# Hybrid diffusion step on one core: layer 0's S5 preparation in S5's own pages and banks, S5's output left where it is made, the retention's values elsewhere

## The chip, the cores and the metric

The kernel runs on one core of a Trainium2 chip. The metric is the device time of one execution in microseconds (us). The core has five engines that work side by side, each through its own queue in a fixed order: TensorE (PE: matmuls and transposes), VectorE (DVE), ScalarE (ACT), GpSimd (POOL), and SyncE (SP), which issues the DMAs here. SBUF is the on-chip memory, PSUM the accumulator memory of TensorE with eight banks.

## The reference

A backbone of two layers runs over two request groups at once: a prompt of 128 tokens and a sample of 512, side by side as 640 columns. Each layer modulates a normed input, projects it once, hands slices of the projection to four mixers, joins their outputs in one projection, and adds a gated feed-forward network.

```python
mod = silu(cond) @ mod_w + mod_b                 # six shifts, scales, gates
h = rmsnorm(x, norm1_w) * (1 + sc1) + sh1
pa, pb, pc, pd = split(h @ w_in)
ya, st_a = ssd_mixer(pa, ...)                    # chunked scan, two directions
yb, st_b = retention_mixer(pb, ...)              # chunked decay attention, two directions
yc, st_c = s5_mixer(pc, ...)                     # complex diagonal scan
yd, st_d = lru_mixer(pd, ...)                    # gated diagonal scan
x = x + g1 * (concatenate([ya, yb, yc, yd]) @ w_out)
h = rmsnorm(x, norm2_w) * (1 + sc2) + sh2
x = x + g2 * conv_ffn(h, ffn_w_up, ffn_conv_w, ffn_conv_b, ffn_w_down)
```

S5 is the mixer that the change is about. Its state matrices follow from parameters alone (`lam`, `log_step`, `b`, `c`), so they can be worked out before any input is there:

```python
step = exp(log_step); mag = exp(lr * step)
abar = mag * (cos(li * step) + 1j * sin(li * step))
bbar = (abar - 1) / lam * b
x = complex_diag_scan(abar, einsum(u, bbar), init)       # both directions
y = real(einsum(x, c)) + d_skip * u
val, gate = split(y @ glu_w);  out = val * sigmoid(gate)
```

The outputs are both groups' final hidden states and the new states of the four mixers.

## The kernel before

Activations lie with features on the partitions and the 640 tokens along the free axis, in two halves of 320. Products of float32 are made of three matmuls: each operand is split into a high part of reduced precision and the rest (names `hi`, `lo`; for the normed input `hhi`, `hlo`), and a tile is the sum of high by high, high by low and low by high. A tile of the input projection is 2 x 8 x 3 such matmuls of 320 columns, named `mm<-hhi,hi` and so on.

**Pages and banks.** SBUF work space is cut into pages of one size under tags, and PSUM into banks under tags; `page(tag)` and `paged(tag, shape, name)` take the next page of a tag, `bank(tag)` the next bank:

```python
PAGES = {"A": 12, "B": 12, "C": 12, "Ya": 2, "Yb": 2, "Yc": 2, "Yd": 2, "H": 16}
BANKS = {"mm": 3, "a": 1, "b": 2, "c": 1, "mod": 1}
```

A is used by the LRU mixer, B by S5, C by SSD; Ya, Yb, Yc and Yd hold the outputs of LRU, SSD, S5 and retention. Bank a serves the LRU, b S5 and the retention, c SSD, mm the large products. A scheduler sets the order of each engine's queue ahead of the run, by program order as priority; the helper `call` (its line is 92, and every instruction of the trace has that line) adds one rule: the first instructions on the tiles of one tag come in program order. So a stage that takes pages of a tag early in the program also comes ahead of every later stage that takes pages of this tag.

**Layer 0's mixers.** In `layer`, the S5 input is projected first (`u`), then `s5_prep(0)` is written out, and then the steps of the mixers in the order of `ORDER[0]`. The prep makes powers of the poles (`pw`, `apcw`), tables (`tab`, stored to DRAM as `tb`), and, in four rounds of four groups, `pmr`/`pmi` from `bb`, their transposes (`wbs`, stored as `wb`), the products `kt` and `kk` with `cm`, and `pmr`/`pmi` from `cq` (stored as `wc`). At its end `dg` is made of `kk`, and both are stored as `zz`. The mixer loads them back in eight scans q0 to q7: matmuls `b<-s5u,wb`, products with the tables (`s5a<-b,tb` on VectorE), two scan instructions (`s5r<-tb,s5a`), products back, then matmuls with `wc`. After q7 come the transposes into `s5y`, the gated unit (`b<-s5y,glu`, tanh into `glut`), and the output.

The other names: `lgw` are LRU's gate matmuls, `gb` its gelu gate; `sxc`, `scb`, `sE`, `xk`, `ssq` belong to SSD, with `z` its gate and `yssd` its output; `rq`, `rv`, `ktok`, `qe`, `rM` belong to the retention; `mod<-mraw` are the modulation's matmuls, written as fillers over the whole mixer stage. The mixers' outputs are split into `yhi` and `ylo`, and the first matmul `mm<-yhi,hi` begins the output projection: first LRU and S5, then SSD and retention.

Of the kernel before, what the change touches and what calls it, by code (L numbers as in the profile page):

```python
# [29 lines left out]
NF = 22  # L30
TB = 81
SK = 2
PB = "c"
EXTRA = ''
TBA = 1
PCP = 1
# [2 lines left out]
TSR = 1  # L39
LB = 1  # L40
FPS = 2
ST = 'AAC'
MR = 'C'

ORDER = ("s5 gb lru lru gb ssd ssd z lru ssd z ret ret ssd ret ssd ret ret ret ret",
# [30 lines left out]
def hybrid_kernel(ctx: ExitStack, tc: tile.TileContext, I, O, dbg=None):  # L76
# [33 lines left out]
    V, G, A, T, SP = Eng(nc.vector), Eng(nc.gpsimd), Eng(nc.scalar), Eng(nc.tensor), Eng(nc.sync)  # L110
# [15 lines left out]
    def page(tag, dt=F32, name="pg"):  # L126
        t = pgp.tile([P, PGB if tag == "B" else PGW], dt, tag=tag, name=name, bufs=PAGES[tag])
        fresh[t.tensor.name] = tag
        return t

    def paged(tag, shape, name, dt=F32):
        n = int(np.prod(shape))
        t = page(tag, dt, name)[:, :n]
        if len(shape) == 1:
            return t
        names = "abcd"[:len(shape)]
        return t.rearrange(f"p ({' '.join(names)}) -> p {' '.join(names)}", **dict(zip(names[1:], shape[1:])))

    def bank(tag):
        t = psp.tile([P, 512], F32, tag=tag, name=tag, bufs=BANKS[tag])  # L140
        fresh[t.tensor.name] = tag
        return t
# [43 lines left out]
    def wsplit(ap, n, cut=512, le=None, tag=None):  # L186

        out = []
        for c0 in range(0, n, cut):
            w = min(cut, n - c0)  # L190
            raw = wp.tile([P, 512], F32, tag="raw", name="raw", bufs=RAWS)
            SP.dma_start(raw[:, :w], ap[:, c0:c0 + w])
            if tag:
                hi, lo = page(tag, F32R, "whi")[:, :512], page(tag, F32R, "wlo")[:, :512]
            else:
                hi = wp.tile([P, 512], F32R, tag="hi", name="hi", bufs=SPLITS)
                lo = wp.tile([P, 512], F32R, tag="lo", name="lo", bufs=SPLITS)
            A.copy(hi[:, :w], raw[:, :w])
            lo_i[0] += 1
            (le or lo_eng[lo_i[0] % len(lo_eng)]).tensor_tensor(lo[:, :w], raw[:, :w], r2f(hi[:, :w]), op=ALU.subtract)  # L200
            out.append((c0, c0 + w, hi, lo))
        return out
# [11 lines left out]
    def col_tile(w, act, nk=8, width=128, halves=(0, 1), col=None, ks=None, out=None):  # L214

        col = col or (lambda k: k * width)
        some = ks or range(nk)
        old = sec[0]
        sec[0] = old + "*"
        out = [out] if out is not None else [bank("mm") for _ in halves]  # L220
        for c0, c1, hi, lo in w:
            ks = [k for k in some if c0 <= col(k) < c1]
            for ps, h in zip(out, halves):
                o, n = HALF[h]
                for k in ks:
                    c = slice(col(k) - c0, col(k) - c0 + width)
                    mm3(ps[:width, :n], hi[:, c], lo[:, c], act[k][0][:, o:o + n], act[k][1][:, o:o + n],
                        k == 0, k == nk - 1)
        sec[0] = old
        return out  # L230
# [261 lines left out]
    M_, A_, S_ = ALU.mult, ALU.add, ALU.subtract  # L492
# [99 lines left out]
    def s5_prep(l):  # L592

        wb, wc, tb, zz = s5d[l]
        p1, p2, p3 = "CCC" if l else ST

        def keep(name, shape):
            return smp.tile([P] + shape, F32, tag=f"k_{name}", name=name)
# [19 lines left out]
        tp = paged(p1, [2, 2, 16, 4], "pwt")  # L618
# [3 lines left out]
        for n in (1, 2, 4):  # L622
            v, o = pwp[:, :, :, 1:1 + n], pwp[:, :, :, 1 + n:1 + 2 * n]
            b = pwp[:, :, :, n:n + 1]
            t, u = [tp[:, i, :, :, 0:n] for i in range(2)]
# [38 lines left out]
            G.tensor_copy(s5x0[l][DH[d], :, :, d].rearrange("p g i -> p i g"), x0[DH[d]])  # L664
        yield


        ek = [u8]
        for k in range(1, 6):
# [4 lines left out]
        for q in range(2):  # L674
            o = 8 * q
# [4 lines left out]
            for k in range(6):  # L680
                n = 1 << k
# [7 lines left out]
            for h in range(2):  # L689

                rv = paged(p1, [4, 2, TB], "tbr")
                for i in range(2):
                    t = tab[i][:, 4 * h:4 * h + 4, :]
# [25 lines left out]
             [bb[:, i] for i in range(2)], [bt[:, i] for i in range(2)])  # L719
        ncq = paged(p2, [16, 16], "ncq")  # L720
        V.tensor_scalar(ncq, cq[:, 1], -1.0, None, op0=M_)
        cm = [paged(p2, [16, 32], f"cm{i}") for i in range(2)]
        for i, c in enumerate((cq[:, 0], ncq)):
            G.memset(cm[i], 0.0)
            for d in range(2):
# [5 lines left out]
        for q in range(4):  # L731
            o = 4 * q
# [15 lines left out]
            for i in range(2):  # L748
                ps = bank("c" if l else PB)
                for k in range(4):  # L750
# [3 lines left out]
                for a in range(2):  # L754
                    SP.dma_start(wb[2 * q + a].rearrange("p (g i c) -> p g i c", g=2, i=2)[:, :, i, :], wbs[:, a])
            ps = bank("c" if l else PB)
            for i in range(2):
# [4 lines left out]
            A.copy(kt, ps[:, 0:128])  # L762
            ps = bank("c" if l else PB)
            T.transpose(ps[:, 0:128], kt, idn)
# [26 lines left out]
    def s5_mixer(l, hh, y, steps):  # L791
# [3 lines left out]
        for i in range(2):  # L795
# [9 lines left out]
            ps = bank("b")  # L805
# [3 lines left out]
            ps = bank("b")  # L809
            for k in range(2):  # L810
                for j in range(2):
                    o = 256 * k + 128 * j
# [111 lines left out]
        for i in range(2):  # L924
            tp = page("B", name="glut")
            for h in range(2):
                o, n = HALF[h]
                t = tp[:, o:o + n]
                for vg in (1, 0):
                    ps = bank("b")  # L930
                    for k in range(2):
                        m = 256 * vg + 128 * i
                        T.matmul(ps[:, :n], gw[k][:, m:m + 128], yt[k][:, o:o + n], start=k == 0, stop=k == 1)
                    if vg:
                        A.activation(t, ps[:, :n], AF.Tanh, scale=0.5)
                    else:
                        V.scalar_tensor_tensor(t, t, 1.0, ps[:, :n], op0=A_, op1=M_)
                G.tensor_scalar(y[i][:, o:o + n], t, 0.5, None, op0=M_)


    def lru_mixer(l, hh, y):
# [296 lines left out]
    def ret_mixer(l, hh, y):  # L1238
# [60 lines left out]
        kx = rotated(13)  # L1299
        yield  # L1300
        units = wsplit(I["w_in"][l, 14], 1024) + wsplit(I["w_in"][l, 15], 1024)
        vk = [paged("B", [5, 128], "rv") for _ in range(2)]
        for c0 in (0, 2, 4):
            n = min(2, 5 - c0)
            ps = bank("b")
            old = sec[0]
            sec[0] = old + "*"
            for c in range(n):
                for k in range(8):
                    hi, lo = units[k // 2][2:]  # L1310
                    w = slice((k % 2) * 256, (k % 2) * 256 + 256)

                    mh, ml = [v[:, 128 * (c0 + c):128 * (c0 + c) + 128] for v in hh[k]]
                    o = ps[:, 256 * c:256 * c + 256]
                    T.matmul(o, mh, hi[:, w], start=k == 0, stop=False)
                    T.matmul(o, mh, lo[:, w], start=False, stop=False)
                    T.matmul(o, ml, hi[:, w], start=False, stop=k == 7)
            sec[0] = old
            for i in range(2):
                A.copy(vk[i][:, c0:c0 + n], ps[:, 0:256 * n].rearrange("p (c w) -> p c w", w=256)[:, :, 128 * i:128 * i + 128])  # L1320
# [16 lines left out]
        for t in range(2):  # L1337
            sq, sp = page("A", name="rsq"), page("A", name="rsp")
            for h in range(2):
                o, n = HALF[h]  # L1340
                ps = bank("b")
# [3 lines left out]
                ps = bank("b")  # L1345
# [14 lines left out]
    def layer(l, norm):  # L1360
# [3 lines left out]
        for ks in steps or (range(8),):  # L1364
            if l == 0 and ks[0]:
                mod_first(ks[0] // 2)
            for h in HO:
                norm.apply(l, 0, h, hh, ks)
        normed = hold[1]
        ys = {n: [page(tag, name="y" + n) for _ in range(2)] for n, tag in (("lru", "Ya"), ("ssd", "Yb"), ("s5", "Yc"))}  # L1370
        ys["ret"] = []
        gens = {"s5": s5_mixer(l, hh, ys["s5"], steps), "lru": lru_mixer(l, hh, ys["lru"]), "ssd": ssd_mixer(l, hh, ys["ssd"]),
                "ret": ret_mixer(l, hh, ys["ret"]), "gb": gates(l, hh, (2, 3), ys["lru"], AF.Gelu_apprx_tanh),
                "z": gates(l, hh, (9, 11), ys["ssd"], None if TSZ else AF.Silu)}
        for n in gens:
            if n != "ret":
                step(n + str(l), gens[n])
            if l == 0 and n == "s5":
                step("s50", gens[n])
                sec[0] = "prep"  # L1380
                for i, _ in enumerate(s5_prep(0)):
                    if i == 1:

                        hold[0] = normed
                hold[0] = None
# [45 lines left out]
        for h in HO:  # L1431
            for m in range(8):
                if m not in us:
                    us[m] = wsplit(I["w_o2"][l, m], 512, tag="C" if m < 4 else None)
                ps = pss.pop(m) if m in pss else col_tile(us[m], act, nk=4, halves=(h,))[0]
# [3 lines left out]
        f = 0  # L1439
# [4 lines left out]
        for gi, gn in enumerate(GRP):  # L1444
            aa = []
            if gi == 1 and l + 1 < L:
                prep = s5_prep(l + 1)
            sec[0] = f"up{l}"
            for k in range(gn):
# [7 lines left out]
                c = page("Yb", name="fc")  # L1457
# [8 lines left out]
                for h in range(2):  # L1466
                    o, n = HALF[h]
# [18 lines left out]
            for m, hs in [(m, (0, 1)) for m in range(8 - n2)] + [(m, (h,)) for h in HO for m in range(8 - n2, 8)]:  # L1486
# [3 lines left out]
                for h, ps in zip(hs, pss):  # L1490
                    residual(m, h, ps, modT[l][5])
                    if last:
                        norm.add(m, h, tail=l + 1 == L and h == HO[1])
                        if l + 1 == L:
                            o, n = HALF[h]
# [23 lines left out]
    for l in range(L):  # L1519
        norm = layer(l, norm)  # L1520
    sec[0] = "fin"
    for i, h in enumerate(HO):
        o, n = HALF[h]
        for k in range(8):
            t = x[k][:, o:o + n]
# [218 lines left out]
```

## Time and profile before

| | |
|---|---|
| median of 3 runs | 1762.29 us (1761.71 to 1763.96) |
| the profiled execution | 1760.15 us, its span 1758.3 us |
| mean granted clock of TensorE | 0.971 |
| PE, DVE, ACT, POOL busy | 94%, 59%, 40%, 27% of the span |
| layer 0's mixers, to the first `yhi` matmul | about 61 to 340 us |
| layer 1's mixers, to its first `yhi` matmul | about 916 to 1185 us |

The span is the profiled execution from its first instruction to its last. Busy shares are averages over stages, so the windows of a stage say more than the page. A row of windows gives, behind the stretch and its length, the busy time and (x) the number of instructions of PE, PEld (weight loads), DVE, ACT and POOL, then the clock that was granted to TensorE (1.00 is full), the DMA share and the GB/s. Matmul durations overlap their neighbours' in the pipeline, so a price of one is read from start to start.

### The profile page before, as it was taken

The page shows a single profiled execution, that of the slowest core. Times are in us where ns is not written, and L with a number is a line of the kernel's source. Part 1 is how long each engine was busy: PE and PEld are TensorE (multiplying, and loading weights), DVE is VectorE, ACT ScalarE, POOL GpSimd, SP SyncE. Part 2 cuts the span into 40 slices and gives each one's busy share as a digit, 9 for nine tenths or more (in the row PEclk, how much of TensorE's full clock was granted, in tenths as well). Part 3 has the DMA queues.
Part 4 walks back from the last instruction along what each step waited for, and adds up shares of the span by engine and source line. Part 5 has one row for each costly group of instructions (what it writes and reads, how often), then busy time and mean ns, then how long its engine had stood idle before and what let it go on. Part 6 is the DMA issues. An engine that isn't in the chain of part 4 may idle for free.

```text
span 1758.3 us, 30749 instructions
## 1 busy us (share of the span) xinstructions
PE 1659.0 (94%) x11342; PEld 1532.9 (87%) x11342; DVE 1042.9 (59%) x2482; ACT 712.0 (40%) x1566; POOL 466.2 (27%) x652
## 2 busy tenths in 40 slices
PE   7877999999999999999988999899999999999997
PEld 3655787888999999999988889798889999999996
DVE  7776976977433773455367678588753343334345
ACT  5724534645321343332335364555453233233244
POOL 2221343413211211221223244432332111211222
PEclk9977999999999999999999999999999999999998
DMA  9465564321435445543333334422112222222321
GB/s 323 148 203 144 176 204 135 90 75 49 125 124 164 152 159 182 184 144 114 97 94 129 113 103 135 144 76 75 37 60 61 79 84 64 88 76 60 94 73 61
DMA packets 143433, 206.50 MB, mean 117 GB/s; under 512 B 22852, under 2 KB 64692, under 8 KB 143284
## 3 DMA queue, kind: packets, MB, share of 16 engines
q1 hardware_dynamic: 143284, 204.54, 37.3%
q8 instruction: 90, 1.47, 0.3%
q14 instruction: 59, 0.48, 0.1%
HBM read 184.42 MB, written 20.07 MB: 116 GB/s over the span
## 4 chain that ended last, share of the span: by engine, by line
PE 77%; DVE 10%; DMA 4%; ACT 3%; issue 3%; POOL 2%; SPq 0%; DVEq 0%; POOLq 0%; ACTq 0%
PE mm L92 65%; PE b L92 6%; PE mod L92 4%; PE c L92 2%; DMA mraw<-in_mod_w 1%; DVE nt L92 1%; DVE x L92 1%; DVE s5r L92 1%; PE a L92 1%; DVE lo L92 1%; POOL lo L92 1%; DVE nsq L92 1%; DMA wb<-wb 1%; ACT hhi L92 1%; DVE sE L92 1%
## 5 line engine op out<-in xcount | busy, mean ns | idle before, releaser
L92 PE MATMUL mm<-hhi,hi 128*128 128x320 f32 x1976 | 624.0, 317 | 17.1 <-ACT hhi L92 11.1
L92 PE MATMUL mm<-hlo,hi 128*128 128x320 f32 x1976 | 622.5, 315 | 5.5 <-POOL hlo L92 2.9
L92 PE MATMUL mm<-hhi,lo 128*128 128x320 f32 x1976 | 617.6, 314 | 0.3 <-DVE lo L92 0.3
L92 ACT CAST hi<-raw 128x512 fp32r<-128x512 f32 (+1 forms) x384 | 227.2, 593 | 594.6 <-PE mm L92 358.5
L92 POOL TENSOR_TENSOR lo<-raw,hi 128x512 fp32r<-128x512 f32 (+1 forms) x200 | 258.0, 1291 | 675.1 <-ACT hi L92 615.3
L92 PEld LDWEIGHTS mm<-hhi,hi 128*128 128x128 f32 x1976 | 375.3, 190 | 37.1 <-ACT hhi L92 16.0
L92 PEld LDWEIGHTS mm<-hlo,hi 128*128 128x128 f32 x1976 | 375.3, 190 | 15.4 <-POOL hlo L92 5.5
L92 PEld LDWEIGHTS mm<-hhi,lo 128*128 128x128 f32 x1976 | 374.9, 190 | 4.3 <-issue 2.2
L92 DVE TENSOR_TENSOR lo<-raw,hi 128x512 fp32r<-128x512 f32 (+1 forms) x184 | 127.3, 692 | 210.3 <-ACT hi L92 202.4
L92 DVE SCALAR_TENSOR_TENSOR x<-mm,mod,x 128x320 f32<-128x320 f32 (+2 forms) x288 | 117.4, 435 | 208.5 <-PE mm L92 206.9
L92 PE MATMUL mm<-fal,hi 128*128 128x320 f32 x640 | 197.4, 309 | 0.0
L92 PE MATMUL mm<-fah,lo 128*128 128x320 f32 x640 | 197.3, 309 | 0.0
L92 PE MATMUL mm<-fah,hi 128*128 128x320 f32 x640 | 195.2, 311 | 0.2 <-DVE x L92 0.2
L92 PEld LDWEIGHTS mm<-fah,hi 128*128 128x128 f32 x640 | 119.2, 188 | 5.4 <-issue 2.5
L92 PEld LDWEIGHTS mm<-fah,lo 128*128 128x128 f32 x640 | 120.4, 188 | 0.4 <-issue 0.4
L92 PEld LDWEIGHTS mm<-fal,hi 128*128 128x128 f32 x640 | 120.4, 188 | 0.0
L92 DVE TENSOR_TENSOR fa<-fc,mm 128x128 f32<-128x128 f32 x132 | 45.2, 373 | 98.1 <-PE mm L92 92.5
L92 PE MATMUL mod<-mraw,s 128*32 128x256 f32 x768 | 69.2, 415 | 18.7 <-DMA mraw<-in_mod_w 18.1
L92 DVE SCALAR_TENSOR_TENSOR fc<-fraw,par,fc 128x643 f32<-128x643 f32 x88 | 81.1, 923 | 2.8
L92 PE MATMUL mm<-yhi,hi 128*128 128x320 f32 x192 | 60.6, 317 | 1.6 <-DVE rg L92 1.1
L92 PE MATMUL mm<-ylo,hi 128*128 128x320 f32 x192 | 60.8, 317 | 1.2 <-DVE ylo L92 1.2
L92 PE MATMUL mm<-yhi,lo 128*128 128x320 f32 x192 | 61.1, 318 | 0.0
(350 smaller groups left out, 2425.7 us busy)
## 6 DMA issues: line engine op xcount, KB each, us to landing
raw<-in_up SPq DMA_DIRECT2D x176, 256.0 KB
mraw<-in_mod_w SPq DMA_DIRECT2D x160, 256.0 KB
raw<-in_w_in SPq DMA_DIRECT2D x80, 256.0 KB
raw<-in_dn SPq DMA_DIRECT2D x96, 192.0 KB
mraw<-in_mod SPq DMA_DIRECT2D x32, 256.0 KB
raw<-in_w_o SPq DMA_DIRECT2D x32, 256.0 KB
tb<-tb SPq DMA_DIRECT2D x16, 326.0 KB
x<-in_x SPq DMA_DIRECT2D x16, 320.0 KB
```

The source lines that it names most:

```text
L92: r = f(*a, **k)
```

## The change

Layer 0's prep took A pages for its powers and tables and for what is made of `bb` (`ST`, its first two letters), C pages for its four rounds (the third letter), and SSD's bank c (`PB`). Now only the first block, up to `apcw`, is on A; everything after it is on S5's B pages, `cm` on S5's two Yc pages, and the transposes and products of the rounds in banks b. S5's output is halved in place and stays in the B pages of `glut`, rather than go to Yc; the retention's values `vk` (`rv`) go to Yc instead of B, in both layers, and their matmuls to a bank mm instead of b. Layer 1's prep stays on C and bank c.

```diff
-PB = "c"
+PB = "b"
-ST = 'AAC'
 def s5_prep(l):
-        p1, p2, p3 = "CCC" if l else ST
+        p1, p2, p3, pc = ("C", "C", "C", "C") if l else ("A", "B", "B", "Yc")
...
+        p1 = p2
...
-        cm = [paged(p2, [16, 32], f"cm{i}") for i in range(2)]
+        cm = [paged(pc, [16, 32], f"cm{i}") for i in range(2)]
 def s5_mixer(l, hh, y, steps):
-                G.tensor_scalar(y[i][:, o:o + n], t, 0.5, None, op0=M_)
+                G.tensor_scalar(t, t, 0.5, None, op0=M_)
+            y.append(tp)
 def ret_mixer(l, hh, y):
-        vk = [paged("B", [5, 128], "rv") for _ in range(2)]
+        vk = [paged("Yc", [5, 128], "rv") for _ in range(2)]
-            ps = bank("b")
+            ps = bank("mm")
 def layer(l, norm):
-        ys = {n: [page(tag, name="y" + n) for _ in range(2)] for n, tag in (("lru", "Ya"), ("ssd", "Yb"), ("s5", "Yc"))}
-        ys["ret"] = []
+        ys = {n: [page(tag, name="y" + n) for _ in range(2)] for n, tag in (("lru", "Ya"), ("ssd", "Yb"))}
+        ys["s5"], ys["ret"] = [], []
```

As a consequence the queues change. The rows below are the queues' instructions in order; the changed kernel's helper has line 91. First PE in the middle of the prep's four rounds. Before (round one of the rounds, then the first scan's matmuls q0, then the next projection tile):

```order
L92 MATMUL mod<-mraw,s_84 32x256 x4
L92 MATMUL c<-ct,pmi 128x128 x4
L92 MATMUL c<-pmr,cm_1015 32x128 x4
L92 MATMUL c<-pmi,cm_1016 32x128 x4
L92 MATMUL mod<-mraw,s_84 32x256 x4
L92 MATMUL c<-ct,kt 128x128
L92 MATMUL b<-s5u,wb 128x81 x4
L92 MATMUL mm<-hhi,hi 128x320
L92 MATMUL mm<-hlo,hi 128x320
L92 MATMUL mm<-hhi,lo 128x320
```

After, the second round's last product `kt`, with the projection's matmuls on both sides:

```order
L91 MATMUL mm<-hhi,hi 128x320
L91 MATMUL mm<-hlo,hi 128x320
L91 MATMUL mod<-mraw,s_84 32x256 x4
L91 MATMUL mm<-hhi,lo 128x320
L91 MATMUL b<-ct,kt 128x128
L91 MATMUL mm<-hhi,hi 128x320
```

What stood back to back with the modulation's fillers now has tiles of LRU, SSD and retention between its matmuls, and the first scan has left the stretch. Next VectorE at the first scan (`s5a<-b,tb`, then `s5r<-tb,s5a`). Before, it lies within the rounds, whose `pmr` and `pmi` are around it:

```order
L92 TENSOR_TENSOR s5a<-b,tb 128x4x81
L92 TENSOR_TENSOR s5a<-b,tb 128x324
L92 TENSOR_TENSOR pmi<-pmi,pt_1083 128x512
L92 SCALAR_TENSOR_TENSOR lxc<-lraw,par_75,lxc 128x643
L92 TENSOR_TENSOR s5a<-s5a 128x2x81 x2
L92 TENSOR_TENSOR lo<-raw,hi 128x512
L92 SCALAR_TENSOR_TENSOR lxc<-lraw,par_75,lxc 128x643
L92 SCALAR_TENSOR_TENSOR s5r<-tb,s5a 64x328 x2
L92 TENSOR_TENSOR s5r<-s5r,tb 128x324
L92 TENSOR_TENSOR s5r<-s5r,s5a 128x2x81
```

After, it stands behind the prep's last step `dg`, with LRU's `lg` and the retention's rotation `rq` between:

```order
L91 TENSOR_TENSOR dg<-dg,kk 16x256
L91 TENSOR_TENSOR rsw<-rsw,rsin 128x512
L91 TENSOR_TENSOR dg<-dg,dq 16x256
L91 TENSOR_TENSOR rq<-rq,rsw 128x512
L91 TENSOR_TENSOR lg<-lg 128x644
L91 TENSOR_TENSOR lo<-raw,hi 128x512
L91 TENSOR_TENSOR s5a<-b,tb 128x4x81
L91 TENSOR_TENSOR s5a<-b,tb 128x324
L91 TENSOR_TENSOR s5a<-s5a 128x2x81 x2
L91 SCALAR_TENSOR_TENSOR s5r<-tb,s5a 64x328 x2
L91 TENSOR_TENSOR s5r<-s5r,tb 128x324
L91 TENSOR_TENSOR s5r<-s5r,s5a 128x2x81
```

All eight scans have moved behind `dg`. Last PE at the last scans. Before, the matmuls of a scan stand between full tiles of the projection:

```order
L92 MATMUL mm<-hhi,hi 128x320
L92 MATMUL mm<-hlo,hi 128x320
L92 MATMUL b<-s5r,wc 128x81 x2
L92 MATMUL b<-s5u,wc 128x81
L92 MATMUL b<-s5r,wc 128x81 x2
L92 MATMUL mm<-hhi,lo 128x320
L92 MATMUL mm<-hhi,hi 128x320
```

After, the scans q6 and q7 stand among SSD's chain (`c<-sxs,btok`, `a<-sE,xk`, `a<-scb,S`), with no tile of the projection between:

```order
L91 MATMUL b<-s5r,wc 128x81 x2
L91 MATMUL b<-s5u,wc 128x81
L91 MATMUL b<-s5r,wc 128x81 x2
L91 MATMUL b<-s5u,wb 128x81 x4
L91 MATMUL c<-sxs,btok 128x128 x4
L91 MATMUL a<-sE,xk 64x128 x2
L91 MATMUL a<-scb,S 128x128
L91 MATMUL b<-s5u,wb 128x81 x2
L91 MATMUL b<-s5r,wc 128x81 x2
L91 MATMUL b<-s5u,wc 128x81
L91 MATMUL b<-s5r,wc 128x81 x2
L91 MATMUL a<-scb,S 128x128
```

SSD's work of the second direction has moved ahead of S5's gated unit, and the projection's tiles that filled the scans of before have gone further ahead or behind.

## Rows read from the trace of the kernel before

**Rows 1.** The page: busy times, PE and its granted clock by slices, chain by engine.

```profile
PE 1659.0 (94%) x11342; PEld 1532.9 (87%) x11342; DVE 1042.9 (59%) x2482; ACT 712.0 (40%) x1566; POOL 466.2 (27%) x652
...
PE   7877999999999999999988999899999999999997
...
PEclk9977999999999999999999999999999999999998
...
PE 77%; DVE 10%; DMA 4%; ACT 3%; issue 3%; POOL 2%; SPq 0%; DVEq 0%; POOLq 0%; ACTq 0%
```

**Rows 2.** Windows of layer 0's mixers, core 0; the columns are named below.

```profile
80.00:100.00 20.00, 9.80 (x75) 6.30 (x73) 16.33 (x32) 10.62 (x29) 2.37 (x9) 0.67 0.73 230
100.00:120.00 20.00, 17.01 (x108) 14.91 (x102) 8.97 (x18) 5.95 (x14) 3.30 (x6) 0.73 0.71 217
120.00:140.00 20.00, 13.55 (x108) 7.93 (x106) 19.64 (x32) 7.32 (x17) 6.35 (x4) 0.87 0.55 163
140.00:160.00 20.00, 13.16 (x79) 6.40 (x71) 5.62 (x13) 7.65 (x16) 0.34 (x7) 0.54 0.56 162
160.00:180.00 20.00, 20.00 (x139) 18.68 (x138) 18.20 (x31) 10.31 (x18) 8.15 (x18) 1.00 0.46 123
180.00:220.00 40.00, 38.03 (x262) 31.80 (x265) 38.10 (x96) 21.84 (x45) 11.36 (x25) 1.00 0.54 168
220.00:260.00 40.00, 39.51 (x300) 35.16 (x300) 28.17 (x62) 12.37 (x31) 16.55 (x26) 1.00 0.65 205
260.00:300.00 40.00, 36.94 (x254) 31.48 (x254) 23.90 (x62) 22.22 (x62) 16.75 (x22) 1.00 0.47 149
300.00:340.00 40.00, 37.58 (x274) 33.60 (x273) 37.50 (x80) 23.38 (x62) 18.40 (x19) 1.00 0.35 101
```

**Rows 3.** Timeline rows (start us, us, engine, line, operation) of PE and SyncE's queue.

```profile
58.23 0.31 PE L92 MATMUL mm<-hhi,hi 128*128 128x320 f32 x1
58.38 0.31 PE L92 MATMUL mm<-hlo,hi 128*128 128x320 f32 x1
...
158.42 0.59 SPq L92 DMA_DIRECT2D zz<-dg  x1
...
262.69 2.39 PE L92 MATMUL b<-s5y,glu 128*128 128x320 f32 x8 [0.48 <-DMA glu<-in_glu]
...
340.01 0.39 PE L92 MATMUL mm<-yhi,hi 128*128 128x320 f32 x1
```

**Rows 4.** PE's waits, 60 to 180 us (total, times, longest).

```profile
PE mod L92 <- DMA mraw<-in_mod_w: 18.1, 7, 6.8
PE c L92 <- DVE pmr L92: 2.5, 2, 2.2
```

**Rows 5.** VectorE's waits, 60 to 340 us.

```profile
DVE dg L92 <- ACT kk L92: 9.4, 1, 9.4
```

**Rows 6.** ScalarE's groups, 60 to 430 us (busy, mean ns, idle before).

```profile
L92 ACT ACT_TABLE_LOAD x7 | 9.0, 1283 | 0.1
```

**Rows 7.** Windows of the old order's stretches, the columns as in rows 2.

```profile
86.70:183.80 97.10, 72.68 (x481) 54.09 (x481) 69.15 (x129) 38.66 (x78) 19.40 (x43) 0.75 0.58 174
183.80:247.40 63.60, 61.14 (x434) 51.88 (x434) 52.08 (x118) 26.88 (x60) 23.06 (x46) 1.00 0.61 190
262.70:340.00 77.30, 72.29 (x507) 63.03 (x508) 58.77 (x137) 43.64 (x119) 32.45 (x37) 1.00 0.40 121
```

**Rows 8.** Tiles of bb and s5a on VectorE (ns min/median/max, first and last start).

```profile
L92 DVE TENSOR_TENSOR bb<-bq,cf x2: 418/422/427, 86.7 to 87.0; 128x256 f32<-128x256 f32 x2
...
L92 DVE TENSOR_TENSOR s5a<-b,tb x16: 458/486/496, 106.8 to 247.8; 128x324 f32<-128x324 f32 x16
```

**Rows 9.** VectorE's groups, 60 to 340 us.

```profile
L92 DVE TENSOR_TENSOR_SCAN s5r<-tb,s5a 64x328 f32<-64x328 f32 x16 | 15.2, 952 | 1.4 <-POOL s5a L92 0.9
...
L92 DVE TENSOR_TENSOR s5a<-b,tb 128x324 f32<-128x324 f32 x16 | 7.1, 487 | 4.8 <-PE b L92 4.8
```

**Rows 10.** PE's waits in layer 1's mixers, 900 to 1303 us.

```profile
PE b L92 <- ACT ktok L92: 4.0, 1, 4.0
```

## The prediction

> **What bounds the kernel now.** I read the page first. TensorE (PE) is busy 94% of the span and 77% of the chain that ended last [rows 1], so a change pays only where PE is idle or slowed. The line of PE by slices is full from the fifth slice on, and its clock line has its lowest digits at the very start [rows 1]. The windows then show where the hole is [rows 2]: in layer 0's mixers, from 80 to 160 us, PE is busy 9.80 + 17.01 + 13.55 + 13.16 = 53.5 of 80 us, at granted clocks of 0.67, 0.73, 0.87 and 0.54. So 26.5 us are idle, and of the busy time 9.80 x 0.33 + 17.01 x 0.27 + 13.55 x 0.13 + 13.16 x 0.46 = 15.6 us is lost to the clock. From 160 us to the first matmul of the output projection, the first one that reads yhi, at 340.0 us [rows 3], PE is busy nearly all the time at clock 1.00 (20.00 of 20, 38.03, 39.51, 36.94 and 37.58 of 40). VectorE (DVE) has two faces there: 95% busy in 180 to 220, 74% in 220 to 260 [rows 2].
>
> What PE waits for between 60 and 180 us is read from the waits [rows 4]: 18.1 us stand at the modulation's weights (mod), which are fillers that the scheduler put there for want of other work, and 2.5 us at the prep's pmr. In this stretch the preparation of S5 (tables, transposes, the products kt and kk) holds LRU's A and SSD's C pages and SSD's bank c, so the LRU's and SSD's tiles, which PE could compute, come after it. The longest wait of DVE is of the same kind: 9.4 us at dg for kk, the prep's last step [rows 5].
>
> **What the change does, part by part.** Instruction counts hardly move; what moves is the order. (1) The prep goes through S5's own B pages and b banks. LRU's, SSD's, z's and retention's tiles no longer stand behind it: PE has these matmuls between the prep's small ones. (2) S5's scans use B pages and b banks too, and tiles of a tag come in order. So all eight scans now stand behind the end of the prep, where before the first two ran inside it. The store of dg stands ahead of the first load of wb in SyncE's queue, so the scans wait for dg as well. (3) The matmuls of retention's values go to a bank mm, their result to Yc, and S5's output stays in B. (4) Four more activation tables are loaded, 1283 ns each [rows 6], on an engine that is 40% busy [rows 1]: nothing while it has gaps, 5 us if all four fell between the last scan and the output, where I see only one or two. I take 0.
>
> The sum follows the path prep, first scan (q0), last scan (q7), glu, first yhi matmul.
>
> **To q0.** The instructions that stand on PE ahead of q0 in the changed order, from 61 us on (both orders are alike up to there), come to 117.4 us at full clock. Prices are by start-to-start steps: 0.148 us for a 320-column matmul [rows 3], 0.118 us for a 256-column one by its columns (320 to 256 at the same rate), and 0.54 us for a glu matmul (two records each; 8 records took 2.39 us, the latency of the first among them [rows 3]). As a check, the same prices give 71.2 us between the first glu and the first yhi matmul of the old order, whose window shows 72.29 us busy [rows 7]. DVE's rows from bb (86.7 us [rows 8]) to q0's first product come to 91.8 us by the means of their groups, of which two are shown [rows 9]. These means overlap a little: the old order's rows from bb to the third scan make 76.9 us, the window shows 69.15; from there to the last scan 56.1 against 52.08 [rows 7]. So I scale by 0.90 and 0.93: 82.6 us on DVE. Dense, PE would bring q0 at 61 + 117.4 = 178 us and DVE at 86.7 + 82.6 = 169 us. PE decides. At the 93% that the old order has from 180 to 200 and around (38.03 of 40 is 95%, 36.94 of 40 is 92% [rows 2]) q0 comes at 61 + 117.4 / 0.93 = **187 us**. The prep's own chain doesn't forbid it: in the old order dg was stored at 158.4 us [rows 3] in spite of the page waits, and the old wait of 9.4 us for kk [rows 5] now has other work in it.
>
> **q0 to q7.** DVE's rows between them come to 80.3 us, scaled 74.5; PE's to 57.6 us. So DVE is the bound there, not PE. DVE reached 38.10 of 40 us (95%) with three of the scans in it [rows 2], and 82% where PE was the bound (52.08 of 63.6 [rows 7]). I take 92%, nearer to the first, since there is less PE work in the way: 81 us, and q7 at **268 us**, about 20 us later than the 247.8 us of before [rows 8].
>
> **q7 to yhi.** In the old order the first glu matmul follows q7's second product by 262.7 - 247.8 = 15 us [rows 3, 8]; I keep that: glu at 283 us. Behind it PE now has only 39.3 us of work up to yhi (16 glu matmuls, SSD's last norms, one of the retention's directions, 120 matmuls of the input projection), where before it had 71.2: the rest has gone ahead of it. At 94% (37.58 of 40, 300 to 340 [rows 2]) that is 42 us: yhi at **325 us** rather than 340.0.
>
> **The sum.** 15 us at yhi. Of PE's work 219.4 rather than 216.2 us now stand ahead of yhi, so 3 us less follow: 18. Layer 1's prep is untouched; there only the retention's values change their bank, and SSD's last norm comes about 30 matmuls (4.4 us) nearer to its reader. The price is at least 0 and at most about the largest wait of PE on retention's side in that layer, 4.0 us [rows 10]; I take 1, as the retention's own end still comes later than SSD's. So 17 us less, 1743 us against the profiled execution's 1760.15 us. The median of the runs is 1762.29, 2 us above it, and I put the forecast between: **1744 us**. A difference of 0.2% (3.5 us) is about what a measurement of this kernel can tell from no change.
>
> **The clock.** In the row of 140 to 160 us PE is busy 13.16 of 20 us at a granted clock of 0.54, close to the lower level (1.2 GHz); it had been idle before, at the mod waits [rows 2, 4]. From q0 to q7 the changed order leaves PE 57.6 us of work in 81 us, 71%, little above that row's 66% and the 68% of 120 to 140, whose clock is 0.87. If PE fell to 0.73, as from 100 to 120, 57.6 / 0.73 = 79 us would still fit into the 81; at 0.54 it needs 107 and becomes the bound, which is the third rival below. The Trainium skill, in "TensorE: Matmul & The Clock Gate", Part 1, says the same of the direction: the clock gate halves the array's clock after idleness and restores it after sustained busy work. This case's rows agree with that direction; by that rule alone the gap's loss of clock would move to the scan stage rather than vanish.
>
> **The rivals.**
> - *Dense* (chance 0.15). The two engines keep 97% or more, as from 160 to 180 us (PE 20.00, DVE 18.20 of 20): q0 at 182, q7 at 259, yhi at 315, a gain of 25 + 3 - 1: about 1733 us. For it: that stretch has scans and LRU work side by side. Against: it lasts 20 us only.
> - *The late scans become the bound* (0.20, the other side). Eight scans one behind the other, each a chain from PE through DVE, POOL, DVE and back, share DVE's queue with SSD's chain; every wait of one delays the other. At 78% of DVE and q0 at 195: q7 at 290, glu at 305, yhi at 347, 7 us later, 4 after the 3 that no longer follow; with 2 in layer 1, 1766 us. It decides where q7 comes after 285: below 76% of DVE in the scan stage with q0 at 187, below 83% with q0 at 195. For it: 220 to 260 had 28.17 of 40, 70%. Against: PE was full then, 39.51 of 40 [rows 2].
> - *A cold clock in the scan stage* (0.07). 107 instead of 81 us at 0.54 throughout, of which a half is likely, as the projection's blocks of 18 and 30 matmuls lie between: 13 us of the 17 are lost, 1756 us.
> - *The hole only moves* (0.10). The 42 us of idleness and lost clock from 80 to 160 come back between 190 and 290, where PE's share falls: no change within 0.2%.
> - The forecast itself has the rest, 0.48.
>
> **Range and chances.** The forecast's own range is 1738 to 1752 (scan stage at 96% to 87%, and 3 us for q0). To hold 8 in 10 it must reach into the dense and the late case: 1730 to 1765. Faster by over 0.2%: the forecast's case nearly whole, the dense case and half of the cold one, 0.65. Within 0.2%: 0.14. Slower: 0.21.
>
> **What would show it.** Right: windows from 80 to 160 with PE at 18 or more of 20 us at clock 1.00; all eight scans between about 187 and 270 us; PE's share down to about 70% there with DVE above 90%; first yhi matmul near 325. The steps are wrong if q0 comes after 195 (the prep on B pages is held by its stores or by evacuations of other tiles), if the scans stand more than 12 us apart, or if more than 45 us pass between glu and yhi. The FFN stages and layer 1 should not differ by more than some us; if they do, something else than this order has changed.

## The result and the profile after

The changed kernel is slower: a median of 1783.55 us over 4 runs (1781.01 to 1785.05) against 1762.31 us beside it, a ratio of 1.0118 with an interval of 1.01 to 1.0135. The forecast was 1744 us. The profiled execution took 1785.05 us, span 1783.3, which is 25.0 us more than before; 24.1 of them are there at the first yhi matmul of layer 0 (364.1 instead of 340.0 us). The profiled execution is the slowest of the four, and that of before lies 2 us under its median: the two times are 24.9 us apart, the medians 21.2.

The windows of layer 0's mixers after the change, columns as in [rows 2]:

```profile
80.00:100.00 20.00, 16.82 (x113) 14.30 (x112) 14.30 (x54) 17.20 (x50) 1.92 (x2) 0.93 0.72 218
100.00:120.00 20.00, 18.31 (x142) 13.37 (x140) 13.01 (x30) 12.85 (x27) 1.57 (x8) 0.99 0.62 206
120.00:140.00 20.00, 18.66 (x145) 16.01 (x145) 18.64 (x31) 14.01 (x26) 7.95 (x13) 1.00 0.48 145
140.00:160.00 20.00, 19.11 (x140) 16.25 (x138) 20.00 (x33) 11.12 (x22) 6.89 (x5) 1.00 0.57 173
160.00:180.00 20.00, 19.40 (x152) 16.75 (x151) 19.69 (x38) 11.96 (x23) 6.59 (x9) 1.00 0.66 209
180.00:220.00 40.00, 36.13 (x248) 31.99 (x247) 26.26 (x51) 11.77 (x32) 12.58 (x22) 0.87 0.45 129
220.00:260.00 40.00, 28.83 (x204) 23.52 (x203) 28.41 (x77) 11.93 (x37) 14.20 (x24) 0.87 0.63 199
260.00:300.00 40.00, 29.11 (x165) 26.74 (x165) 31.58 (x84) 17.57 (x50) 13.59 (x27) 0.74 0.39 113
300.00:340.00 40.00, 30.92 (x133) 23.58 (x134) 27.03 (x78) 20.58 (x46) 11.45 (x13) 0.78 0.37 123
```

The hole from 80 to 160 us is filled as forecast: PE is busy 72.9 of 80 us instead of 53.5, at a clock of 0.93 to 1.00. A larger one has opened from 220 to 340 us: PE is busy 88.9 of 120 us there at clocks of 0.74 to 0.87, where [rows 2] have 114.0 of 120 at 1.00. The landmarks on VectorE show when (tile rows with first and last start, two of before and then those after the change), and two rows of PE's timeline show the ends:

```profile
L92 DVE MEMSET tab<- x4: 65/65/65, 60.8 to 72.7; 128x8 f32 x4
L92 DVE TENSOR_TENSOR dg<-dg,dq x1: 414/414/414, 154.6 to 154.6; 16x256 f32<-16x256 f32 x1
```

```profile
L91 DVE TENSOR_TENSOR bb<-bq,cf x2: 417/420/424, 100.5 to 101.2; 128x256 f32<-128x256 f32 x2
L91 DVE STREAM_TRANSPOSE s5u<-b x6: 407/442/451, 68.6 to 74.6; 128x256 f32<-128x256 f32 x6
L91 DVE MEMSET tab<- x4: 65/65/65, 73.7 to 84.3; 128x8 f32 x4
L91 DVE TENSOR_TENSOR dg<-dg,dq x1: 406/406/406, 192.2 to 192.2; 16x256 f32<-16x256 f32 x1
L91 DVE TENSOR_TENSOR s5a<-b,tb x16: 457/486/496, 201.4 to 296.2; 128x324 f32<-128x324 f32 x16
```

```profile
313.34 0.70 PE L91 MATMUL b<-s5y,glu 128*128 128x320 f32 x2
...
364.15 0.39 PE L91 MATMUL mm<-yhi,hi 128*128 128x320 f32 x1
```

bb, at 86.7 us in [rows 8], comes at 100.5; the prep ends at 192 us rather than 155 (dg); the scans run from 201.4 to 296.2; glu follows at 313.3, yhi at 364.1. The longest waits of VectorE and of PE from 195 to 364 us are for loads (total, times, longest):

```profile
DVE s5a L91 <- DMA tb<-tb: 12.8, 2, 6.8
DVE s5a L91 <- PE b L91: 6.9, 4, 5.5
```

```profile
PE b L91 <- DMA wc<-wc: 8.6, 2, 5.1
PE mod L91 <- DMA mraw<-in_mod_w: 7.0, 3, 5.2
PE b L91 <- DMA wb<-wb: 4.8, 2, 2.9
```

PE's idle time, and the time that it lost to the clock (busy time multiplied by one less the granted clock, in windows of 10 us), can be added up between the landmarks, so that the stretches differ in length. In us, idle + clock, from 60 us to dg: 27.0 + 12.4 us before, 7.7 + 2.6 after. From dg to glu: 2.9 + 2.0 before, 28.8 + 19.3 after. From glu to yhi: 5.0 + 0.0 before, 6.2 + 3.7 after. So 29 us were gained in the first part and 48 lost in the other two.

### The profile page after: what moved, and what is told of

It is laid out like the page before. It is cut to its first block, busy times and chain, and to the rows that moved or that the text cites. A ratio compares the mean times of both kernels' runs of the same rounds, so it can differ in the third digit from the quotient of the medians.

```text
span 1783.3 us, 30724 instructions
## 1 busy us (share of the span) xinstructions
PE 1677.8 (94%) x11342; PEld 1556.2 (87%) x11342; DVE 1039.0 (58%) x2482; ACT 717.3 (40%) x1570; POOL 471.8 (26%) x652
## 4 chain that ended last, share of the span: by engine, by line
PE 77%; DVE 10%; DMA 4%; issue 3%; ACT 3%; POOL 2%; SPq 1%; DVEq 0%; POOLq 0%; ACTq 0%
PE mm L91 65%; PE b L91 5%; PE mod L91 3%; PE c L91 1%; PE a L91 1%; DVE x L91 1%; DVE nt L91 1%; DMA mraw<-in_mod_w 1%; DVE s5r L91 1%; DMA scb<-cumd 1%; DVE nsq L91 1%; DVE sE L91 1%; DVE lo L91 1%; SPq L91 1%; POOL lo L91 1%
## 5 line engine op out<-in xcount | busy, mean ns | idle before, releaser
L91 PE MATMUL mod<-mraw,s 128*32 128x256 f32 x768 | 65.6, 402 | 13.2 <-DMA mraw<-in_mod_w 12.4
```

The costliest lines, as they stand in the source:

```text
L91: r = f(*a, **k)
```

## The experiments

The table gives for each kernel the ratio to the kernel before on the same chip (interval), and in its trace the start of dg, the first and last product of the scans with their tables, the first glu and the first yhi matmul, in us. Each time of the table is read from one execution; that of f2 is its fastest of ten, that of e6 its slowest of four. Theory 1: the page squeeze on B makes the prep late, and the scans with it. Theory 2: the scans wait for their loads. Rival 4: SSD's chain stands between the scans. By the scan stage is meant the time from the first to the last of these products.

| | ratio | dg | scans | glu | yhi |
|---|---|---|---|---|---|
| before | 1 | 154.6 | 106.8 to 247.8 | 262.7 | 340.0 |
| changed | 1.0118 (1.01 to 1.0135) | 192.2 | 201.4 to 296.2 | 313.3 | 364.1 |
| e1 prep only | 1.0165 (1.0144 to 1.0185) | 195.6 | 203.8 to 291.5 | 306.4 | 368.7 |
| e2 the rest only | 0.9989 (0.9977 to 1.0001) | 155.4 | 107.6 to 248.8 | 265.7 | 338.9 |
| e3 bank only | 1.0017 (1.0002 to 1.0032) | 145.0 | 142.3 to 249.6 | 266.1 | 344.9 |
| e4 rounds on C | 1.0041 (1.0024 to 1.0058) | 177.2 | 169.3 to 270.1 | 283.2 | 345.7 |
| e5 six tiles on A | 1.0078 (1.0063 to 1.0093) | 161.7 | 175.8 to 281.0 | 296.9 | 355.4 |
| e6 scan loads, ACT | 1.0101 (1.0078 to 1.0124) | 196.3 | 196.7 to 298.8 | 317.0 | 371.9 |
| e8 rounds on C, bank c | 1.0054 (1.0037 to 1.007) | 179.8 | 121.3 to 269.9 | 292.0 | 352.4 |
| e9 one set of loads | 0.9999 (0.9984 to 1.0013) | 194.1 | 202.7 to 263.5 | 282.6 | 345.8 |
| e10 the same on before | 1.0053 (1.0032 to 1.0074) | 151.9 | 106.3 to 219.7 | 241.1 | 335.6 |
| e11 wb, wc on Yd | 1.0418 (1.0397 to 1.0438) | 190.8 | 200.9 to 280.6 | 299.4 | 356.6 |
| e12 SSD last | 1.0354 (1.0326 to 1.0381) | 189.5 | 197.9 to 259.9 | 269.5 | 358.4 |
| f1 SSD loads, ACT | 1.0124 (1.0099 to 1.0149) | 191.3 | 205.3 to 302.6 | 315.5 | 365.2 |
| f2 pages, no loads | 1.0025 (1.001 to 1.004) | 192.8 | 200.5 to 256.9 | 276.3 | 340.3 |
| g1 scan loads, POOL | 1.0179 (1.0146 to 1.0213) | 192.8 | 193.1 to 308.4 | 326.2 | 373.7 |

**Which part.** e1 is the change without the lines on S5's output and the retention's values, with `("A", "B", "B", "B")`; e2 is those lines alone.

> Only the preparation moves: layer 0's prep on S5's B pages and banks b, with cm on B too; S5's output (Yc), the retention's values (B) and their bank (b) are as before. Theory 1 (the prep's four rounds are squeezed into the B pages that are left, so they end late and all eight scans run behind them, with too little other PE work beside them): nearly the whole loss of 21 us stays, 1776 to 1786 us, first scan near 200 us, last near 295. Rival (the retention's values and S5's output, by their new pages and bank, cost the time): 1755 to 1766 us.

> Only the rest of the change: S5's output stays in its B pages, the retention's values go to Yc and their matmuls to a bank mm; the prep is as before. Theory 1: within 4 us of before, 1758 to 1766 us. Rival (these pages and this bank cost the time): 1775 to 1785 us.

The prep alone costs more than the whole (1791.48 us, 5 us above what theory 1 allowed); the rest alone costs nothing and may give 2 us. The loss is the prep's.

**Pages or banks.** e3 is the kernel before with one line changed; e4 and e8 are the changed kernel with the rounds back on C, e8 with the bank back as well.

```diff
-PB = "c"
+PB = "b"
```

```diff
-        p1, p2, p3, pc = ("C", "C", "C", "C") if l else ("A", "B", "B", "Yc")
+        p1, p2, p3, pc = ("C", "C", "C", "C") if l else ("A", "B", "C", "Yc")
```

> Only the bank: layer 0's prep uses the banks b, its pages stay A, A and C. The banks alone put all eight scans behind the prep's last transpose, but the rounds keep their 12 C pages. Theory 1 (pages): the prep ends about as early as before (kk near 155 us), 1758 to 1770 us. Rival 2 (the order of the banks b, that is, scans behind the prep by itself, is what costs): 1775 us or more.

> The whole change, but the four rounds take their pages from C as before (the first block on A, the tables and the products of b and c on B, cm on Yc, bank b). Theory 1: with 12 pages to turn over in, the rounds end 35 to 40 us of PE work earlier than in the changed kernel, the scans start near 170 us, and LRU is free of the prep all the same: 1745 to 1762 us. Rival 2 (scans behind the prep by the order of the banks): 1770 us or more.

> The whole change, but the rounds take C pages and bank c as before; only the tables and the products of b and c moved to B. The first two scans run inside the rounds again. Theory 1 (late scans): 1752 to 1764 us, since the scans are as early as in the kernel before or nearly so, and LRU is free of the tables. Rival (what costs is LRU's tiles in front of the prep on shared engines): still 1768 or more, as in the run with the rounds on C and bank b (1770).

e3 puts all eight scans behind the rounds by the bank's order alone, and it is slower by 0.02 to 0.32%: that order by itself isn't the cause. e4 takes about 14 of the 21 us back, but at 1770.24 us it is above theory 1's range; e8, with its first scan at 121 us, has 1772.24, where its rival (LRU's tiles ahead of the prep on engines that both use) put it, not theory 1. So with rounds and bank as before, moving the tables and what is made of b and c to B still costs about 10 us; by what way was not tried. Both have their hole back at 120 to 160 us: PE is busy 26.91 and 25.16 of 40 us there, before 26.71.

**The squeeze on B.** e5 takes the six tiles made from b and c to A, so that the rounds have more B pages.

```diff
+        pk = "C" if l else "A"
...
-        bq, cq = paged(p2, [2, 16, 16], "bq"), paged(p2, [2, 16, 16], "cq")
+        bq, cq = paged(pk, [2, 16, 16], "bq"), paged(pk, [2, 16, 16], "cq")
...
```

> The whole change, but the six tiles that the prep makes from b and c ahead of its rounds (bq, cq, bb, bt, ncq, kk; four of them live to the prep's end) are on A pages instead of B, so the four rounds have about ten B pages to turn over in instead of about six. Theory 1 (page squeeze on B delays the rounds and with them all scans): dg comes 25 us earlier than in the changed kernel (192 to about 165), the first scan near 172 instead of 201, the last near 262 instead of 296, and the time falls to 1750 to 1766 us. Rival (the delay comes from VectorE and ScalarE, which LRU's and SSD's tiles now share with the prep): dg stays above 182, 1774 us or more.

dg came at 161.7 us, 30 us earlier, as theory 1 has it; the time fell by 7 us only, to 1776. The edit does two things: on A, bb no longer stands behind the tables and begins at 64.5 us, so the first round (its first pmr) begins 10 us earlier, at 93.6 instead of 103.8; and from there to dg it takes 68.1 us instead of 88.4. In these two stretches (windows of e5, then of the changed kernel) VectorE has 53.95 and 80.16 us of work, so other stages' work has left the rounds:

```profile
93.60:161.70 68.10, 56.79 (x417) 45.19 (x417) 53.95 (x111) 37.16 (x76) 7.35 (x18) 0.89 0.60 184
103.80:192.20 88.40, 84.07 (x637) 70.06 (x632) 80.16 (x149) 50.02 (x96) 26.08 (x39) 1.00 0.54 163
```

More work stands in the scans instead. They take 105 us from first to last, with PE busy 92.17 of them, where the changed kernel has 72.64 of 94.8; in e4 it is 98.81 of 100.8 (windows of e5 and of e4):

```profile
175.80:281.00 105.20, 92.17 (x639) 79.39 (x638) 78.60 (x174) 45.24 (x112) 41.36 (x66) 0.91 0.56 175
169.30:270.10 100.80, 98.81 (x728) 91.31 (x726) 81.86 (x187) 37.00 (x91) 42.12 (x63) 0.99 0.55 169
```

So the prep's lateness isn't the whole of the loss: theory 1 holds for the prep and falls for the time.

**The loads.** e6 issues the scans' loads from ScalarE's queue in both layers, g1 from GpSimd's in layer 0, f1 issues layer 0's loads of SSD's `scb` from ScalarE's; e9 loads one set of matrices for all eight scans of layer 0, f2 does the same but still takes and returns the pages; e11 moves two pages of each scan of layer 0 to Yd. Of e6 and e9 one place each:

```diff
-            SP.dma_start(wbt[:, 0:512], wb[q])
+            A.dma_start(wbt[:, 0:512], wb[q])
...
```

```diff
-            wbt, tbt = page("B", name="wb"), page("B", name="tb")
...
+            if q and l == 0:
+                wbt, tbt = one
+            else:
+                wbt, tbt = page("B", name="wb"), page("B", name="tb")
+                one[:] = [wbt, tbt]
...
```

> The whole change, but the scans' loads (wb, its block of zz, tb, wc) are issued from ScalarE's queue instead of SyncE's, both layers. Rival 3 (the scans wait for loads that stand behind other transfers and waits in SyncE's queue: 12.8 us at tb, 8.6 at wc, 4.8 at wb in the changed kernel): the scan stage shrinks from 95 to 75 us or less and the time falls by 15 us or more, to 1768 or less. Theory 1: these waits are symptoms of scans that are late all together; less than 10 us fall, 1775 to 1786 us.

> The changed kernel, but layer 0's eight scans load wb, tb and wc once, for the first scan, and all use that set (so the other seven scans compute with the first one's matrices). No load and no page of a load stands between the scans any more. Theory 2 (in the scan stage each scan waits for loads whose B pages come free only when an earlier scan is done): the stage, first to last scan, falls from 95 us to 70 or less, glu comes at 285 or earlier instead of 313, the time is 1760 or less. Rival 4 (the scan stage is long because SSD's chain stands between the scans in the in-order queues): the stage stays above 80 us and the time above 1770.

> The same edit on the kernel before, as the control: there TensorE is busy 97% of the scan stage, so nothing should come of it by either theory but what the shorter chain lets the scheduler move: within 8 us of before, 1754 to 1764 us.

> The changed kernel with the scans' wb and wc pages of layer 0 on the two Yd pages, which are empty until the retention's output, so that each scan takes three B pages instead of five. Theory 2: the waits for tb, wb and wc shrink by half or more, the scan stage is 75 to 85 us, the time 1765 to 1776. Rival 4: less than 5 us, 1778 or more.

> The changed kernel with layer 0's ten loads of scb (SSD's decay rows) issued from ScalarE's queue, so that the scans' loads no longer stand behind them in SyncE's queue. Theory 2a (the queue couples the two chains): first to last scan falls from 95 to 80 us or less, the time to 1772 or less. Theory 2b (the B pages come free late): the stage stays above 88 us, the time above 1777.

> As the run with one set of loads for all scans, but each scan still takes its pages for wb, tb and wc and gives them back when it did before (they are only touched, not loaded; the scans compute with the first one's matrices). Theory 2a (the queue, or the transfers themselves): the same as with one set, within 4 us, 1758 to 1766. Theory 2b (pages): back towards the changed kernel, 1772 or more.

> The changed kernel with layer 0's scan loads (wb, tb, wc and their blocks of zz) issued from GpSimd's queue, where no other load stands. Theory 2a' (they are late because of what stands ahead of them in SyncE's queue): the scan stage falls from 95 to 80 us or less, the time to 1772 or less. Theory 2c (the transfers themselves, 966 KB for each scan, are what each scan waits for): the stage stays above 88 us, 1776 or more.

With one set of loads the scan stage falls from 95 to 61 us and the whole loss is gone (1762.03 us). Holding the pages alone doesn't bring it back: in f2 the stage is 56 us. But f2's median of 1768.87 lies between what the two theories foretold, 0.1 to 0.4% above before, so its time decides for neither. Nor is it one queue: on ScalarE's queue the stage is 102 us, on GpSimd's 115, and without SSD's loads ahead of them 97. The control e10, on the kernel before, was expected within 8 us and came out slower by 0.5%, 10 us: its scans take 113 us instead of 141, and its first yhi matmul comes 4 us earlier, but its output projection takes 94 us, from the first to the last `yhi,hi` matmul, instead of 80. So a shorter scan stage isn't a shorter kernel by itself.

e11's stage is 80 us, inside theory 2's range, but its waits for wb, tb and wc, which were to halve, come to 24.4 us against 26.2; and its total of 1838.2 is far off: its output projection stretches to 138 us. Yd is where the retention's output goes; whether that is why was not tried. Three more kernels combined e5 with e6 (1778.9 us), with f1 (1775.61) and with g1 (1780.78), where 1755 to 1765 was foretold for the last two if a queue holds the loads up; e4 with f1 gave 1769.74. None was better than its first half by more than 1 us.

**SSD's chain.** e12 moves SSD's last three steps behind the retention's.

```diff
-ORDER = ("s5 gb lru lru gb ssd ssd z lru ssd z ret ret ssd ret ssd ret ret ret ret",
+ORDER = ("s5 gb lru lru gb ssd ssd z lru z ret ret ret ret ret ret ret ssd ssd ssd",
...
```

> The changed kernel with the order of the mixers' steps altered in layer 0: SSD's last three steps (its chunks) come behind the retention's. Its chain of products no longer stands between the scans. Rival 4: the scan stage is 75 us or less, glu comes at 290 or earlier. Theory 2: the stage stays above 85 us. The total isn't foretold to 10 us by either, since SSD's chain then has to end ahead of the second half of the output projection: 1755 to 1785.

The scans keep all their loads and take 62 us, as with one set of loads. A window of e12 over them, columns as in [rows 2], shows how little is beside them, and that the stage is short at a clock of 0.63:

```profile
198.00:260.00 62.00, 44.40 (x244) 37.30 (x242) 33.33 (x86) 5.84 (x20) 15.82 (x36) 0.63 0.64 197
```

The total is 1827 us: SSD's products begin at 387.9 us only, 29.5 us behind the first yhi matmul, and the output projection, which needs them, takes 127 us. So rival 4 was right on the stage. It also puts e9 and f2 in another light. These are the tile rows of SSD's products on PE, two batches, first of the kernel before, then of the changed one, then of e9; the last row is the first batch of f2:

```profile
L92 PE MATMUL c<-sE,xk x20: 272/298/323, 274.5 to 297.8; 128*64 128x128 f32 x20
L92 PE MATMUL a<-sE,xk x20: 272/298/323, 324.0 to 348.5; 128*64 128x128 f32 x20
```

```profile
L91 PE MATMUL c<-sE,xk x20: 272/421/477, 250.0 to 272.8; 128*64 128x128 f32 x20
L91 PE MATMUL a<-sE,xk x20: 273/421/477, 285.9 to 316.3; 128*64 128x128 f32 x20
```

```profile
L91 PE MATMUL c<-sE,xk x20: 272/420/476, 259.9 to 281.4; 128*64 128x128 f32 x20
L91 PE MATMUL a<-sE,xk x20: 272/323/475, 298.1 to 333.1; 128*64 128x128 f32 x20
```

```profile
L91 PE MATMUL c<-sE,xk x20: 272/421/476, 256.1 to 274.8; 128*64 128x128 f32 x20
```

Before, both batches run after the last scan (247.8 us). After the change both lie inside the scan stage or against glu. In e9 most of the first and all of the second come after the last scan (263.5), in f2 nearly all (last scan 256.9). Is it then the loads, or SSD's products standing behind the scans, that makes these stages short? The time of the fifth scan tells, as none of these products has run before 250 us in the changed kernel, e9, f2 or e12. These are its rows in VectorE's timeline, of the changed kernel, e9, f2, e12 and e1:

```profile
254.81 0.90 DVE L91 TENSOR_TENSOR s5a<-b,tb 128x324 f32<-128x324 f32 x2 [0.22 <-PE b L91]
```

```profile
233.60 0.85 DVE L91 TENSOR_TENSOR s5a<-b,tb 128x324 f32<-128x324 f32 x2
```

```profile
229.07 0.90 DVE L91 TENSOR_TENSOR s5a<-b,tb 128x324 f32<-128x324 f32 x2
```

```profile
239.69 0.90 DVE L91 TENSOR_TENSOR s5a<-b,tb 128x324 f32<-128x324 f32 x2 [0.97 <-PE b L91]
```

```profile
238.59 0.90 DVE L91 TENSOR_TENSOR s5a<-b,tb 128x324 f32<-128x324 f32 x2 [0.67 <-PE b L91]
```

From the first scan to the fifth the changed kernel takes 53 us, e9 31 and f2 29: here, ahead of SSD's products, 22 to 25 us go with the loads. (e12, with its loads but without SSD's chain, takes 42, so SSD's earlier steps count here too.) From the fifth to the last it takes 41 us, beside SSD's products; e9 takes 30, f2 27 and e12, which keeps its loads, 20. So both have a part, the loads in the first scans and SSD's products in the last. e1 fits this, and shows that it isn't the whole: its first stretch takes 35 us, with little waiting for loads, its second 52 us beside SSD's products, which begin at 239.5 us; and it is the slower kernel. By what way a load delays a scan stays open, as neither a queue nor the holding of pages does it by itself.

## Why the prediction was wrong

- **The filled hole** was right: PE 72.9 of 80 us from 80 to 160, though the first window, 16.82 of 20 at 0.93, falls short of the sign that was set.
- **To q0**, forecast 187, measured 201.4. The step took PE's work as what decides, and said that the prep's own chain doesn't forbid it. That is where it failed: the prep's end, dg, came at 192.2 us, and q0 behind it. Two things made dg late. The tables `tab` went to B too, where S5's input (`s5u`, last start 74.6 us) stands ahead of them by the order of the tag: they begin at 73.7 us instead of 60.8, and bb, for which the step had taken 86.7 us, comes 13.8 us late. Every kernel here with the tables on B has them at 73 to 75 us, every one with them on A at 60 to 62. And the rounds, from the first pmr to dg, took 88.4 us (64.8 before), with PE busy 84.07 and VectorE 80.16 us of them. Behind dg come 9.2 us for which the sum had nothing: in SyncE's queue dg's store, three more stores and then the first loads. VectorE waits 6.8 us for tb there. In e6 and g1, whose scan loads are in another queue, q0 comes 0.4 and 0.3 us behind dg. PE's sum was short as well: 126.59 us busy of the 137.20 us to q0's first matmul, at 0.98, where the forecast had 117.4; its share, 92%, is the forecast's 93%.

```profile
61.00:198.20 137.20, 126.59 (x922) 107.92 (x921) 111.94 (x275) 79.26 (x177) 37.83 (x52) 0.98 0.56 170
```

```profile
192.65 0.55 SPq L91 DMA_DIRECT2D zz<-dg  x1
193.25 1.91 SPq L91 DMA_DIRECT2D zz<-kk  x3
195.25 0.54 SPq L91 DMA_DIRECT2D wb<-wb  x1
195.84 0.43 SPq L91 DMA_DIRECT2D tb<-tb  x1
```

- **q0 to q7**, forecast 81 us at 92% of VectorE, measured 94.8 at 72% (68.41 of 94.8 in the first row below). This is the step that failed in kind: a sum of work on two engines was taken as the bound of a stage in which neither is full. The sums themselves were near (VectorE 74.5 forecast; PE 57.6, measured 72.64 x 0.81 = 58.8 at full clock). Two chains, the scans and SSD's chunks, each pass PE, VectorE, ScalarE and GpSimd and wait for loads, in queues of fixed order; e12, e9 and f2 show that the stage is 33 to 38 us shorter without the one or without the loads. That a wait of one chain stops the other is the reading that fits this, not a thing that was measured by itself. The second rival had this mechanism, with 0.20 and 347 us at yhi; it was undersized.
- **q7 to glu**, forecast 15, measured 17.1.
- **glu to yhi**, forecast 42, measured 50.8. PE's work there was 39.3 us by the prices; the second row shows 44.60 busy at 0.90, which is 40.1 at full clock. The rest is idle time and clock, among it 3.91 us at the retention's state (rso). Three of the table loads, which I had costed at nothing, stand back to back with their users, glut and SSD's norms, 3.8 us on ScalarE's side of this stretch (rows below). What they cost isn't shown: of PE's waits here only 1.6 us, at ktok, are for a result that ScalarE makes right behind them.

```profile
201.40:296.20 94.80, 72.64 (x475) 63.61 (x475) 68.41 (x170) 35.80 (x101) 33.80 (x60) 0.81 0.52 163
313.30:364.10 50.80, 44.60 (x248) 37.34 (x247) 26.38 (x54) 23.57 (x44) 17.39 (x17) 0.90 0.21 64
```

```profile
320.92 1.28 ACT L91 ACT_TABLE_LOAD   x1
322.21 0.53 ACT L91 ACTIVATE ssq<-c,c_eps 128x320 f32<-128x320 f32 x1
322.76 1.28 ACT L91 ACT_TABLE_LOAD   x1
324.05 0.44 ACT L91 ACTIVATE glut<-b 128x320 f32<-128x320 f32 x1
324.51 1.28 ACT L91 ACT_TABLE_LOAD   x1
```

The four misses, 14 + 14 + 2 + 9 us, make the 39 us between the forecast 325 and the measured 364. All three signs by which the steps were to be wrong came: q0 after 195, scans 13.5 us apart on average, more than 45 us from glu to yhi.

**Behind yhi** the forecast had 3 us less in layer 0 and 1 us more in layer 1. These are the output projections of the layers, two rows of before and two after the change:

```profile
L92 PE MATMUL mm<-yhi,hi x96: 303/310/549, 340.0 to 420.4; 128*128 128x320 f32 x96
L92 PE MATMUL mm<-yhi,hi x96: 306/310/416, 1185.5 to 1267.1; 128*128 128x320 f32 x96
```

```profile
L91 PE MATMUL mm<-yhi,hi x96: 307/310/550, 364.1 to 440.3; 128*128 128x320 f32 x96
L91 PE MATMUL mm<-yhi,hi x96: 303/309/556, 1200.7 to 1290.0; 128*128 128x320 f32 x96
```

At the end of layer 0's projection the change is 19.9 us behind, so 4.2 us came back there; at the end of layer 1's it is 22.9 us behind, at the end of the span 25.0. The 5.1 us lost on the way are more than the 1 us of the forecast, but 3.7 of them may be the choice of executions, by which the profiled times lie further apart than the medians. One reading of the prediction was wrong without effect: VectorE's share from 220 to 260 us is 70% (28.17 of 40, [rows 2]), not the 74% of its first paragraph.

**The clock** moved with the hole: 0.81 over the scan stage, 0.74 from 260 to 300. The Trainium skill, "TensorE: Matmul & The Clock Gate", Part 1, has the array's clock halved after idleness; the windows agree: 1.00 from 140 to 180 us, where PE was busy 19.11 and 19.40 of 20 us, and 0.74 from 260 to 300, where it was busy 29.11 of 40. A cold clock alone isn't what makes the stage long, as e12's 62 us at 0.63 show.

No version beats the kernel before by more than the measurement can tell; e2 (1761.45 us) comes nearest.

## What to carry to other kernels

Where one long chain of stages (here prep, scans, glu) sets the end of a phase, work that fills an idle engine in its first stage is taken from its later ones and shares their queues: follow the chain's landmarks in the new order, and ask of each stage whether any engine is full in it before a sum of work is taken as its length. A stage in which no engine is full is longer than any engine's sum, and here only traces with and without a neighbour showed by how much. A tile that changes its tag moves behind everything that took this tag earlier, so look for the first instruction of each moved tile, not only for the last.

## What the runs showed of the hardware

The scan stage takes 62 us in e12 at a granted clock of 0.63 and 56 us in f2 at 1.00 (PE's windows from 198 to 260 and from 200 to 257 us), while it takes 95 us in the changed kernel at 0.81. The three differ in loads and neighbours as well, so no run tells what the clock alone costs, but the coldest of them is 33 us shorter than the changed kernel's. How far the steps from engine to engine make its length was not measured by itself.

Moving the 40 loads of the scans from SyncE's queue to GpSimd's, where no other load stands, made q0 come 8 us earlier and the last scan 12 us later, so that the stage is 20 us longer (115 instead of 95). Each issue takes GpSimd 0.55 to 0.76 us among the scans' own instructions, about 24 us for all 40 at 0.6; that this is what lengthens the stage is likely, not shown.
